# Hybrid S5 and gated-linear-attention trunk on one core: where u is scaled, how q is scaled, and the order of the S5 tables

## The chip, the cores and the metric

One core of a Trainium2 chip runs the kernel. The metric is the device time of one execution in microseconds (us), the median of several runs. TensorE is PE, VectorE DVE, ScalarE ACT, GpSimd POOL; SyncE's queue (SP) issues nearly all DMAs.

## The reference

Two layers on x of 512 tokens by 1024 features, f32, then an RMSNorm:

```python
h = rmsnorm(x, norm_mix)
z = h @ w_in                        # u | q | k | v | g | gate_lr
y = s5(u)                           # 32 groups: 16 channels, 64 complex states
y = gelu(y); y = y * sigmoid(y @ w_glu + b_glu)
y_s5 = rmsnorm(y, s5_out_norm)
y_gla = gated_linear_attention(q, k, v, g, gate_lr)   # 4 heads, chunks of 64
x = x + concat(y_s5, y_gla) @ w_out
h = rmsnorm(x, norm_ffn)
x = x + (silu(h @ W1) * (h @ W2)) @ w_ffn_out
```

S5 is a diagonal complex recurrence s_t = a s_(t-1) + B u_t with the output Re(C s_t) + D u_t; D is the skip diagonal `s5_d`. In the attention, q and k are multiplied with exponentials of the summed log gates within a chunk.

## The kernel before

Activations lie with the features on the partitions: x is eight tiles of 128 x 512. The gain of the norm is folded into x; the row factor rstd (one value for each token, R["rstd"]) is multiplied into the results after the projection. Each projection tile (128 outputs by 512 tokens) is 8 blocks of weights by three matmuls (L575), since a product in f32 is made of high and low halves. Weights come in units of 8 blocks: `Weights.ensure` (L156) issues the load on SP (L142), the cast to the high half on ACT (L163, `whi`) and the low half on DVE (L165, `wlo`), two units ahead. There are two buffers of raw weights, so the load of unit v + 2 waits until unit v is split.

The order on PE, ACT and SP is the order in which the program emits (`manual_schedule`); so is the order on DVE in layer 0 up to the v tiles (the region opened at L1139). POOL, and DVE elsewhere, are ordered by the scheduler of the framework by a modelled timeline and by priority.

The mixer of a layer, `mix` (L647), in the order of layer 0:
- `u_pair` (L698): u tiles 0 and 1, the gate's low-rank tile, u tile 2; in the middle of u tile 2 `stats` (L703) makes rstd and rU, rstd's values in the order of S5 (L682). `gate_a` and `gate_c` (L765, L779) make the sums of the log gates.
- u is reordered for S5: `u_copy` (L740) copies 16 blocks of 32 x 128 from PSUM on ACT, then `u_scale` (L737) multiplies with rU on DVE. Tile 3 follows in `u_tile` (L724), with the gate's exponentials (`gate_b`, L791).
- `q_tile` (L802): one multiply with the exponential E (L807), then four of 64 x 256 with rstd (L814) into `qz`, two tiles padded with zeros by POOL (L813). `k_tile`, `g_tile`, `ke_t` follow, then the four v tiles (`v_tiles`, L906), between whose blocks S5 is called through the table at L1161.
- S5 for one tile of u: `s5_fwd` (L829): 8 matmuls with Wk, four DVE multiplies with cosines and sines (L841 to L844), two POOL adds (L846, L847), eight DVE scans (L852). `s5_back` (L859): four DVE multiplies (L866 to L873) and two POOL adds (L869, L874) make sr and sm. `s5_y` (L881): PE matmuls with Tz and Vx, then gelu on ACT (L899).
- `glu`, the S5 part and the attention part of the output projection close the mixer (`TAIL`, L87).

The S5 tables of layer 0 are made beside this in steps. `prep_w` makes Wk: powers of the decay times B, transposed on DVE (L441) and placed by four DMAs each (L446). `prep_v` makes Vx, four complex products on POOL (`cplx`, L404, eight instructions), and Tz with the skip diagonal `idd` (four DVE multiplies of the identity, L498). `prep_rot` makes cosines and sines on POOL (L567 to L572). `bg0` (L1380) says which steps come at which call of `bg`; the calls stand in L708, L730 and L1141 to L1169. Layer 1's tables are made during the feed-forward part of layer 0, its S5 is called from L1109 to L1137, between q, k and g.

All temporary tiles share a pool of NACT = 45 buffers of 128 x 512 (L203).

## Time and profile before

| | us |
|---|---|
| median of three runs | 1160.08 (1159.53 to 1160.54) |
| the profiled execution, its own time | 1159.86 |
| its span, first to last instruction | 1158.1 |
| busy: PE | 1110.1 |
| busy: DVE | 706.2 |
| busy: ACT | 485.6 |
| busy: POOL | 331.9 |

The span is what the profile's rows cover; 1.76 us of the execution's time lie around it. Matmuls overlap each other and their ends are modelled, so a busy PE is not one at its peak. The mixer of layer 0 takes the first 210 us or so, that of layer 1 lies around 605 to 790 us.

### The profile page before, as it was taken

The page shows a single profiled execution, that of the slowest core. Times are in us where ns is not written, and L with a number is a line of the kernel's source. Part 1 is how long each engine was busy: PE and PEld are TensorE (multiplying, and loading weights), DVE is VectorE, ACT ScalarE, POOL GpSimd, SP SyncE. Part 2 cuts the span into 40 slices and gives each one's busy share as a digit, 9 for nine tenths or more (in the row PEclk, how much of TensorE's full clock was granted, in tenths as well). Part 3 has the DMA queues.
Part 4 walks back from the last instruction along what each step waited for, and adds up shares of the span by engine and source line. Part 5 has one row for each costly group of instructions (what it writes and reads, how often), then busy time and mean ns, then how long its engine had stood idle before and what let it go on. Part 6 is the DMA issues. An engine that isn't in the chain of part 4 may idle for free.

```text
span 1158.1 us, 13973 instructions
## 1 busy us (share of the span) xinstructions
PE 1110.1 (96%) x5316; PEld 913.9 (79%) x5316; DVE 706.2 (61%) x947; ACT 485.6 (42%) x844; POOL 331.9 (29%) x322
## 2 busy tenths in 40 slices
PE   8789779999999999999999799999999999999997
PEld 5568658888888888888887688888888888888886
DVE  7996976866454454564466994686545444444454
ACT  6853458443232232432358653745323222222243
POOL 6899544546000052065030440352000000000003
PEclk9899889999999999999999999999999999999999
...
GB/s 211 55 112 126 37 37 37 92 130 116 103 109 100 137 91 101 82 109 91 93 104 41 73 61 85 56 91 94 107 100 85 106 99 102 91 91 109 91 91 73
DMA packets 64099, 107.72 MB, mean 93 GB/s; under 512 B 37408, under 2 KB 38304, under 8 KB 64032
## 3 DMA queue, kind: packets, MB, share of 16 engines
...
q8 instruction: 42, 0.69, 0.2%
q10 hardware_dynamic: 144, 0.26, 0.1%
...
## 4 chain that ended last, share of the span: by engine, by line
PE 79%; DVE 12%; ACT 3%; issue 2%; POOL 2%; DMA 1%; SPq 1%; DVEq 0%; POOLq 0%; ACTq 0%
PE fg L576 7%; PE fg L577 7%; PE fg L578 7%; PE fu L578 7%; PE fu L576 7%; PE fu L577 7%; PE fo L578 7%; PE fo L576 7%; PE fo L577 7%; DVE ro L852 2%; DVE wlo L165 2%; ACT U L745 1%; DVE qz L814 1%; DMA wrr<-in_wr_dram 1%; DMA raw<-in_wst_dram 1%
## 5 line engine op out<-in xcount | busy, mean ns | idle before, releaser
L165 DVE TENSOR_TENSOR wlo<-raw,whi 128x1024 fp32r<-128x1024 f32 x182 | 242.2, 1333 | 113.2 <-ACT whi L163 112.0
L163 ACT CAST whi<-raw 128x1024 fp32r<-128x1024 f32 x183 | 191.8, 1050 | 280.0 <-PE fo L577 116.9
L602 POOL TENSOR_TENSOR sq_fin<-sq_fin 128x512 f32<-128x512 f32 x5 | 6.5, 1296 | 341.8 <-ACT sq_fin L598 341.8
L1237 DVE TENSOR_TENSOR fu<-fu,rs_ffn 128x512 f32<-128x512 f32 x44 | 30.4, 691 | 116.7 <-PE fu L578 113.9
L1254 DVE TENSOR_TENSOR xall<-xall,fo 128x512 f32<-128x512 f32 x78 | 53.1, 686 | 61.9 <-PE fo L578 61.7
L1234 DVE TENSOR_TENSOR fg<-fg,rs_ffn 128x512 f32<-128x512 f32 x44 | 30.3, 688 | 34.7 <-PE fg L578 30.8
L1236 ACT ACTIVATE fg<-fg 128x512 f32<-128x512 f32 x44 | 27.7, 629 | 42.5 <-DVE fg L1234 42.4
L899 ACT ACTIVATE y<-y 32x128 f32<-32x128 f32 x128 | 34.4, 269 | 20.9 <-PE y L890 17.3
L1238 DVE TENSOR_TENSOR fu<-fg,fu 128x512 f32<-128x512 f32 x44 | 31.3, 711 | 5.7 <-ACT fg L1236 1.3
L745 ACT COPY U<-u 32x128 f32<-32x128 f32 x128 | 32.9, 257 | 1.5
L852 DVE TENSOR_TENSOR_SCAN ro<-sp_mag,ro 128x128 f32<-128x128 f32 x64 | 28.5, 507 | 6.6 <-POOL ro L846 6.6
L1089 POOL TENSOR_TENSOR xall<-xall,wo 128x512 f32<-128x512 f32 x16 | 25.5, 1613 | 24.0 <-DVE wo L1088 24.0
L407 POOL TENSOR_TENSOR pt<-bc,sp_a1r 128x256 f32<-128x256 f32 x2 | 1.7, 852 | 94.0 <-issue 92.0
L568 POOL TENSOR_TENSOR rt<-rg 128x512 f32<-128x512 f32 x8 | 10.2, 1288 | 59.8 <-ACT rg L548 59.7
L602 POOL TENSOR_TENSOR sq_s<-sq_s,sq_s 128x512 f32<-128x512 f32 x6 | 8.1, 1342 | 64.3 <-ACT sq_s L598 64.3
L869 POOL TENSOR_TENSOR sr<-ro,ro 128x508 f32<-128x508 f32 x8 | 14.6, 1826 | 39.3 <-DVE ro L867 39.3
L602 POOL TENSOR_TENSOR sq_x1nmix<-sq_x1nmix 128x512 f32<-128x512 f32 x7 | 9.2, 1315 | 57.3 <-ACT sq_x1nmix L598 57.3
L890 PE MATMUL y<-sr,Vx 128*128 128x128 f32 x64 | 15.0, 322 | 8.0 <-POOL sr L869 7.8
L890 PE MATMUL y<-sm,Vx 128*128 128x128 f32 x64 | 14.8, 318 | 6.2 <-POOL sm L874 6.2
L888 PE MATMUL y<-U,Tz 128*128 128x128 f32 x64 | 14.9, 320 | 5.5 <-DVE ro L842 5.4
L846 POOL TENSOR_TENSOR ro<-ro,ro 128x512 f32<-128x512 f32 x8 | 10.7, 1344 | 30.8 <-DVE ro L843 30.8
L890 PEld LDWEIGHTS y<-sr,Vx 128*128 128x128 f32 x64 | 11.9, 231 | 8.9 <-POOL sr L869 8.9
...
## 6 DMA issues: line engine op xcount, KB each, us to landing
...
```

The costliest lines, as they stand in the source:

```text
L163: self.nc.scalar.copy(hi, raw)
L165: (self.nc.gpsimd if v in POOL_W else self.nc.vector).tensor_tensor(lo, raw, hi.bitcast(F32), op=ALU.subtract)
L576: nc.tensor.matmul(ps, whi, xh, start=start, stop=False)
L577: nc.tensor.matmul(ps, whi, xl, start=False, stop=False)
L578: nc.tensor.matmul(ps, wlo, xh, start=False, stop=stop)
L745: nc.scalar.copy(u[32 * t:32 * t + 32, j].rearrange("p (n c) -> p n c", n=NCH), pv[32 * j:32 * j + 32, :, t, :],)
L852: v.tensor_tensor_scan(dst[:, cs], sp["mag4"][:, c:c + 1].to_broadcast([P, P]), src[:, cs], 0.0, M, A)
L890: nc.tensor.matmul(o, Vx[:, pr, part, 1:].rearrange("p a b c -> p (a b c)"), s_[:, cs], start=False, stop=(part == 1),)
L899: nc.scalar.activation(yv[32 * j:32 * j + 32, :, t, :], ps[32 * t:32 * t + 32, j * P:(j + 1) * P].rearrange("p (n c) -> p n c", n=NCH), AF ...
L1237: nc.vector.tensor_tensor(u, pu, rstd[0], op=M)
L1238: nc.vector.tensor_tensor(u, g, u, op=M)
L1254: nc.vector.tensor_tensor(xT[n], xT[n], ps[n], op=A)
```

## The change

- u is scaled at PSUM: `u_scale` multiplies the PSUM tile with rstd on DVE into a new tile `us`, and the 16 ACT copies read `us`. rU is gone. Tiles 0 and 1 are scaled in `stats`, tile 2 after both `gate_c`, tile 3 ahead of `gate_b`.
- q: `gate_d`, called in `q_tile` behind the matmuls, takes the decay of the chunk ends from E and multiplies E with rstd; four instructions then multiply PSUM with 0.125 and E into `qz`. The `qz` tiles are four fixed tiles that are cleared once at startup.
- The skip diagonal is laid out in memory (columns 1024 to 1151 of `s5bc`) and loaded in `prep_load`; `dskip` leaves the small constants.
- The steps of layer 0's tables follow a list of letters, `TABLES` (s small, w Wk, v Vx and Tz, r rotations). The last two pairs of Wk transposes come two calls earlier each; the fourth product of `prep_v` is made on DVE in layer 0.
- S5 of tile 0 is called ahead of the v tiles, and `s5_scan` is a function of its own, called right behind `s5_fwd` at each other place; the S5 adds and small memsets on POOL get high priority. The table of calls between the v blocks and the order behind it are new.
- NACT is 41.

The diff; left out are the renamed columns, the calls of `s5_scan` in layer 1 and the host's layout:

```diff
     pp = ctx.enter_context(tc.tile_pool(name="pp", bufs=1, space=PS))
-    NACT = 45
+    NACT = 41
...
     Tz = cp.tile([P, 16, P], F32, name="Tz")
+    qz = [[cp.tile([P, 4, 2, 64], F32, name=f"qz{hp}{i}") for i in range(2)] for hp in range(2)]
     cosT = cp.tile([P, 16, P], F32, name="cosT")
...
             t = act(f"bc{l}{i}")
-            nc.sync.dma_start(t, s5bc[l][:, 2 * i:2 * i + 2].rearrange("p a b -> p (a b)"))
+            nc.sync.dma_start(t, s5bc[l][:, 512 * i:512 * i + 512])
             bcs.append(t)
-        return bcs, blks or zeros(f"bk{l}")
+        idd = act(f"idd{l}")[:, 0:P]
+        nc.sync.dma_start(idd, s5bc[l][:, 4 * 256:])
+        return bcs, blks or zeros(f"bk{l}"), idd
...
         for n in (1, 2, 3, 4):
-            cplx(e, l, cr, nci, spv(f"a{n}r", l), spv(f"a{n}i", l),
+            cplx(e[n - 1], l, cr, nci, spv(f"a{n}r", l), spv(f"a{n}i", l),
                  halves(Vx[:, :, 0, n]), halves(Vx[:, :, 1, n]), conj=True)
             yield
-        idd = act(f"idd{l}")
-        for b in range(NB):
-            r = slice(32 * b, 32 * b + 32)
-            nc.vector.tensor_tensor(
-                idd[r, 0:P].rearrange("p (a b) -> p a b", a=4),
-                bcast(C("ident")[r, 32 * b:32 * b + 32], [32, 4, 32], 1),
-                bcast(S(l, "dskip")[r, 4 * b:4 * b + 4], [32, 4, 32], 2), op=M,
-            )
-        yield
         ps = psum(f"kt{l}", "aux")
...
-        def unit_rows():
-            rU = R["rU"] = act(f"rU{l}", F32, (P, P))
-            rv = ntc(R["rstd"])
-            for t in range(TS):
-                h = slice(32 * t, 32 * t + 32)
-                nc.vector.tensor_copy(rU[h].rearrange("p (n c) -> p n c", n=NCH), rv[h, :, t, :])
-
-        U = {}
+        U, us = {}, {}
...
                     nc.vector.tensor_tensor(R["r"], R["psr"], R["rstd"], op=M)
-                unit_rows()
+                for b in range(2):
+                    u_scale(b, ps[b])
                 if l == 0:
                     bg()
-                u_evac(0, ps[0])
+                u_copy(0)
                 W.LOOK = 2
...
             gate_a(1)
-            u_copy(1, ps[1])
+            u_copy(1)
             gate_c(0)
             gate_c(1)
-            u_scale(1)
-            u_evac(2, ps2)
+            u_scale(2, ps2)
+            u_copy(2)
...
             ps = dense(lambda k: ("in", k, b * P), f"u{l}{b}")
+            u_scale(b, ps)
             if mid is not None:
                 mid()
-            u_copy(b, ps)
+            u_copy(b)
             if l == 0:
                 bg()
-            u_scale(b)
-
-        def u_evac(b, ps):
-            u_copy(b, ps)
-            u_scale(b)
-
-        def u_scale(b):
-            nc.vector.tensor_tensor(U[b], U[b], bcast(R["rU"], [P, 4, P], 1), op=M)
-
-        def u_copy(b, ps):
+
+        def u_scale(b, ps):
+            t = us[b] = act(f"us{l}{b}")
+            nc.vector.tensor_tensor(t, ps, R["rstd"], op=M)
+
+        def u_copy(b):
             u = act(f"U{l}{b}", F32, (P, 4, P))
-            pv = ntc(ps)
+            pv = ntc(us.pop(b))
             for j in range(4):
...
             nc.scalar.activation(ntc(ee), nct(mn), AF.Exp, scale=1.0 / 16)
+            E[hp] = (e, ei, ee)
+
+        def gate_d(hp):
+            e = E[hp][0]
             d = dec[hp] = cp.tile([P, NCH], F32, tag=f"dec{hp}", name=f"dec{l}{hp}")
             nc.vector.tensor_copy(d, e.rearrange("p (n s) -> p n s", n=NCH)[:, :, 63])
-            E[hp] = (e, ei, ee)
-
-        def q_tile(hp, mid=None):
+            nc.vector.tensor_tensor(e, e, R["rstd"], op=M)
+
+        def q_tile(hp):
             ps = dense(lambda k: ("in", k, O_Q + hp * P), f"q{l}{hp}")
-            if mid is not None:
-                mid()
+            gate_d(hp)
             e = E[hp][0]
-            nc.vector.scalar_tensor_tensor(e, ps, 0.125, e, op0=M, op1=M)
-            qz = [act(f"qz{l}{hp}{i}", F32, (P, 4, 2, 64)) for i in range(2)]
             for i in range(2):
...
                     r = slice(64 * d, 64 * d + 64)
-                    nc.gpsimd.memset(qz[i][r, :, 1 - d], 0.0)
-                    nc.vector.tensor_tensor(
-                        qz[i][r, :, d], e[r, hf].rearrange("p (n t) -> p n t", n=4),
-                        R["rstd"][r, hf].rearrange("p (n t) -> p n t", n=4), op=M,
+                    nc.vector.scalar_tensor_tensor(
+                        qz[hp][i][r, :, d], ps[r, hf].rearrange("p (n t) -> p n t", n=4), 0.125,
+                        e[r, hf].rearrange("p (n t) -> p n t", n=4), op0=M, op1=M,
                     )
-            qd[hp] = qz
+            qd[hp] = qz[hp]
...
             pe = nc.gpsimd
-            pe.tensor_tensor(a1, a1, a2, op=A)
-            pe.tensor_tensor(a3, a3, a4, op=SB)
+            with tc.high_priority():
+                pe.tensor_tensor(a1, a1, a2, op=A)
+                pe.tensor_tensor(a3, a3, a4, op=SB)
+            rot[b] = (a1, a2, a3, a4, co, si)
+
+        def s5_scan(b):
+            a1, a2, a3, a4, co, si = rot[b]
             for dst, src in ((a2, a1), (a4, a3)):
...
                     c = 16 * l + 4 * b + j
-                    v.tensor_tensor_scan(
+                    nc.vector.tensor_tensor_scan(
                         dst[:, cs], sp["mag4"][:, c:c + 1].to_broadcast([P, P]), src[:, cs], 0.0, M, A
                     )
-            rot[b] = (a1, a2, a3, a4, co, si)
...
             sr, sm = act(f"sr{l}{b}"), act(f"sm{l}{b}")
-            nc.gpsimd.memset(v4(sr)[:, :, 0:1], 0.0)
-            nc.gpsimd.memset(v4(sm)[:, :, 0:1], 0.0)
+            pe = nc.gpsimd
+            with tc.high_priority():
+                pe.memset(v4(sr)[:, :, 0:1], 0.0)
+                pe.memset(v4(sm)[:, :, 0:1], 0.0)
             v.tensor_tensor(a1, a2, co, op=M)
             v.tensor_tensor(a3, a4, si, op=M)
-            pe = nc.gpsimd
-            pe.tensor_tensor(
-                v4(sr)[:, :, 1:P], v4(a1)[:, :, 0:P - 1], v4(a3)[:, :, 0:P - 1], op=SB
-            )
+            with tc.high_priority():
+                pe.tensor_tensor(
+                    v4(sr)[:, :, 1:P], v4(a1)[:, :, 0:P - 1], v4(a3)[:, :, 0:P - 1], op=SB
+                )
             v.tensor_tensor(b1, a2, si, op=M)
             v.tensor_tensor(b2, a4, co, op=M)
-            pe.tensor_tensor(
-                v4(sm)[:, :, 1:P], v4(b1)[:, :, 0:P - 1], v4(b2)[:, :, 0:P - 1], op=A
-            )
+            with tc.high_priority():
+                pe.tensor_tensor(
+                    v4(sm)[:, :, 1:P], v4(b1)[:, :, 0:P - 1], v4(b2)[:, :, 0:P - 1], op=A
+                )
             sst5[b] = (sr, sm)
...
             ke_t(1)
+            s5_fwd(0)
             bg()
+            s5_scan(0)
             region.close()
+
+            def s5(b):
+                s5_fwd(b)
+                s5_scan(b)
+
             v_tiles({
-                0: [bg, bg],
-                1: [lambda: s5_fwd(0), bg],
-                2: [lambda: s5_back(0), bg],
-                3: [lambda: s5_fwd(1)],
-                4: [lambda: score(0), lambda: s5_back(1), bg],
-                5: [lambda: s5_y(0), lambda: s5_fwd(2), bg],
-                6: [lambda: s5_y(1), lambda: s5_back(2), lambda: s5_fwd(3)],
-                7: [lambda: score(1), lambda: s5_back(3)],
+                0: [lambda: s5_back(0), bg],
+                1: [lambda: s5(1), bg],
+                2: [lambda: score(0), bg],
+                3: [lambda: s5_back(1), bg],
+                4: [lambda: s5_y(0), lambda: s5(2), bg],
+                5: [lambda: score(1), lambda: s5_back(2), bg],
+                6: [lambda: s5_y(1), lambda: s5(3)],
+                7: [lambda: s5_back(3)],
             })
+            y_split(0)
             s5_y(2)
-            y_split(0)
             y_split(1)
+            g_tile(3)
             y_split(2)
-            g_tile(3)
             s5_y(3)
...
         nc.gpsimd.memset(Tz, 0.0)
+        for t in qz[0] + qz[1]:
+            nc.gpsimd.memset(t, 0.0)
         blks = zeros("bk0")
...
         pw_ = prep_w(0, nc.vector, pl)
-        pv_ = prep_v(0, nc.gpsimd, pl)
+        pv_ = prep_v(0, 3 * [nc.gpsimd] + [nc.vector], pl)
         next(pv_)
...
-        BG_W = (1, 0, 2, 1, 1, 1, 1, 1, 1, 1)
+        TABLES = (
+            "sssvw", "w", "", "ww", "w", "wr", "wwr", "wwr", "wv", "v", "r", "v", "r", "v", "", "v", "v",
+        )
...
             step0[0] += 1
-            if i == 0:
-                drain(small_)
-                next(pv_)
-                next(pw_)
-                return
-            i -= 1
-            for _ in range(BG_W[i] if i < len(BG_W) else 0):
-                next(pw_, None)
-            if i in (2, 3, 10, 12, 13, 14, 15):
-                next(pv_, None)
-            if i in (4, 5, 6, 10, 11):
-                next(rots)
-            if i == 15:
-                drain(pv_)
+            for c in TABLES[i] if i < len(TABLES) else "":
+                next({"s": small_, "v": pv_, "w": pw_, "r": rots}[c], None)
```

## Rows read from the trace of the kernel before

**Rows 1.** The page, first part: busy us, share of the span, instructions.
```profile
PE 1110.1 (96%) x5316; PEld 913.9 (79%) x5316; DVE 706.2 (61%) x947; ACT 485.6 (42%) x844; POOL 331.9 (29%) x322
```

**Rows 2.** Busy time of each engine in three stretches.
```profile
core 0: us, PE busy (x) PEld busy (x) DVE busy (x) ACT busy (x) POOL busy (x), PEclk, DMA share, GB/s
36.00:63.00 27.00, 22.00 (x80) 16.05 (x81) 26.59 (x50) 23.07 (x53) 22.18 (x25) 0.88 0.19 61
104.00:124.00 20.00, 14.69 (x100) 11.71 (x88) 14.72 (x23) 8.42 (x15) 15.68 (x15) 0.98 0.08 27
639.00:680.00 41.00, 33.44 (x181) 28.77 (x180) 40.87 (x69) 22.85 (x59) 19.96 (x20) 0.96 0.19 58
```

**Rows 3.** Timeline, TensorE, 62 to 125 us: three matmuls that waited.
```profile
start us, us, engine line op out<-in xcount [idle before <-releaser]
...
62.38 0.79 PE L578 MATMUL q<-x0h,wlo 128*128 128x512 f32 x1 [2.93 <-DVE wlo L165]
...
71.14 0.50 PE L578 MATMUL k<-x0h,wlo 128*128 128x512 f32 x1 [1.68 <-DVE wlo L165]
...
124.07 0.76 PE L888 MATMUL y<-U,Tz 128*128 128x128 f32 x2 [5.38 <-DVE ro L842]
```

**Rows 4.** Timeline, ScalarE, 30 to 166 us.
```profile
30.74 4.27 ACT L745 COPY U<-u 32x128 f32<-32x128 f32 x16
...
39.39 1.05 ACT L163 CAST whi<-raw 128x1024 fp32r<-128x1024 f32 x1 [3.31 <-DMA raw<-in_wst_dram]
...
45.45 8.59 ACT L745 COPY U<-u 32x128 f32<-32x128 f32 x32
...
55.53 1.05 ACT L163 CAST whi<-raw 128x1024 fp32r<-128x1024 f32 x1
...
67.03 1.05 ACT L163 CAST whi<-raw 128x1024 fp32r<-128x1024 f32 x1
...
71.56 1.06 ACT L163 CAST whi<-raw 128x1024 fp32r<-128x1024 f32 x1 [3.48 <-DMA raw<-in_wst_dram]
...
164.39 0.63 ACT L1001 ACTIVATE th<-g 128x512 f32<-128x512 f32 x1 [2.81 <-DVE g L992]
```

**Rows 5.** Timeline, VectorE, 36 to 75 us, around the gates and the first q tile.
```profile
36.06 0.62 DVE L706 TENSOR_TENSOR rsb<-r,rs_mix 128x512 f32<-128x512 f32 x1
...
58.24 2.37 DVE L738 TENSOR_TENSOR U<-U,rU 128x512 f32<-128x512 f32 x2
...
69.87 1.22 DVE L165 TENSOR_TENSOR wlo<-raw,whi 128x1024 fp32r<-128x1024 f32 x1
...
71.72 3.07 DVE L814 TENSOR_TENSOR qz<-E,rs_mix 64x256 f32<-64x256 f32 x4
```

**Rows 6.** Timeline, VectorE, single prices, and the first S5 multiply.
```profile
44.35 0.42 DVE L407 TENSOR_TENSOR pt<-bc,sp_fr 128x256 f32<-128x256 f32 x1
...
63.92 0.94 DVE L408 TENSOR_TENSOR pt<-bb,sp_a1i 128x256 f32<-128x256 f32 x1
...
99.80 3.95 DVE L498 TENSOR_TENSOR idd<-cst,xall 32x128 f32<-32x128 f32 x4
103.79 0.69 DVE L841 TENSOR_TENSOR ro<-x,cosT 128x512 f32<-128x512 f32 x1
```

**Rows 7.** Timeline, SyncE's queue: the last group of Wk's DMAs, time of issuing.
```profile
96.01 2.71 SPq L446 DMA_DIRECT2D Wk<-wt  x4
```

**Rows 8.** Timeline, GpSimd: startup, and the first S5 add.
```profile
8.83 0.98 POOL L397 MEMSET bk<- 128x512 f32 x2
13.53 6.09 POOL L602 TENSOR_TENSOR sq_x0nmix<-sq_x0nmix 128x512 f32<-128x512 f32 x4 [3.72 <-ACT sq_x0nmix L598]
...
112.49 1.29 POOL L846 TENSOR_TENSOR ro<-ro,ro 128x512 f32<-128x512 f32 x1
```

**Rows 9.** Timeline, VectorE, 113 to 157 us: scans and the last S5 multiply.
```profile
113.81 4.54 DVE L852 TENSOR_TENSOR_SCAN ro<-sp_mag,ro 128x128 f32<-128x128 f32 x4 [4.61 <-POOL ro L846]
...
128.46 3.19 DVE L852 TENSOR_TENSOR_SCAN ro<-sp_mag,ro 128x128 f32<-128x128 f32 x8
...
156.25 0.69 DVE L873 TENSOR_TENSOR rp<-ro,cosT 128x512 f32<-128x512 f32 x1
```

**Rows 10.** Timeline, VectorE, layer 1: a U scale.
```profile
633.86 1.34 DVE L738 TENSOR_TENSOR U<-U,rU 128x512 f32<-128x512 f32 x1 [1.23 <-ACT U L745]
```

More of the change, by code (lines that the diff above doesn't have):

```diff
@@ L50 @@
 for _n, _w in (
-    ("nmix", 8), ("nffn", 8), ("s5n", 4), ("glan", 4), ("bglu", 4), ("bgate", 2), ("dskip", 16),
+    ("nmix", 8), ("nffn", 8), ("s5n", 4), ("glan", 4), ("bglu", 4), ("bgate", 2),
     ("nfin", 8), ("wgate", 256),
@@ L427, in prep_w @@
     def prep_w(l, e, pl):
-        bcs, bk = pl
+        bcs, bk, _ = pl
         bb = act(f"bb{l}")
@@ L483, in prep_v @@
     def prep_v(l, e, pl):
-        bcs, bk = pl
+        bcs, bk, idd = pl
         cr, nci = v3(bcs[1], 0), v3(bcs[1], 1)
@@ L519, in prep_v @@
                 Tz[0:32, sl, 0:32], kv[:, :, 0:32],
-                idd[r, 0:P].rearrange("p (a b) -> p a b", a=4), op=A,
+                idd[r].rearrange("p (a b) -> p a b", a=4), op=A,
             )
@@ L1114, in mix @@
             s5_fwd(1)
+            s5_scan(1)
             k_tile(0)
@@ L1119, in mix @@
             s5_fwd(2)
+            s5_scan(2)
             k_tile(1)
@@ L1123, in mix @@
             s5_fwd(3)
+            s5_scan(3)
             g_tile(0)
@@ L1158, in mix @@
             ke_t(1)
+            s5_fwd(0)
             bg()
+            s5_scan(0)
             region.close()
+            def s5(b):
+                s5_fwd(b)
+                s5_scan(b)
             v_tiles({
[L1162 to L1169 removed]
+                0: [lambda: s5_back(0), bg],
[6 more added lines that the diff above has]
+                7: [lambda: s5_back(3)],
             })
+            y_split(0)
             s5_y(2)
[L1172 removed]
             y_split(1)
+            g_tile(3)
             y_split(2)
[L1175 removed]
             s5_y(3)
@@ L1413, in bg1 @@
                             prep_w(l + 1, nc.gpsimd, side["pl"]),
-                            prep_v(l + 1, nc.gpsimd, side["pl"]),
+                            prep_v(l + 1, 4 * [nc.gpsimd], side["pl"]),
                             prep_rot(l + 1, nc.gpsimd),
@@ L1456, in lay_out @@
     s5bc = np.empty((DEPTH, P, 4, 16, 16), np.float32)
+    skip = np.zeros((DEPTH, P, 4, 32), np.float32)
     for l in range(DEPTH):
@@ L1464, in lay_out @@
         put(l, "bgate", f["gla_b_gate"][l].reshape(2, P).T)
-        put(l, "dskip", np.tile(f["s5_d"][l].reshape(16, 32).T, (TS, 1)))
+        for b in range(NB):
+            for i in range(32):
+                skip[l, 32 * b + i, :, i] = f["s5_d"][l].reshape(NB, 4, 32)[b, :, i]
         s5l[:, 0, l] = gp(f["s5_lam_re"][l])
@@ L1484, in lay_out @@
     putc("reset", (np.arange(L) % 64 != 0)[None])
-    arr = dict(xt=xt, wst=wst, wr=wr, small=small, s5l=s5l, s5bc=s5bc.reshape(DEPTH, P, 4, 256), const=const)
+    arr = dict(xt=xt, wst=wst, wr=wr, small=small, s5l=s5l, const=const)
+    arr["s5bc"] = np.concatenate([s5bc.reshape(DEPTH, P, 1024), skip.reshape(DEPTH, P, P)], 2)
     return {k: np.ascontiguousarray(v, dtype=np.float32) for k, v in arr.items()}
```

## The prediction

> **What bounds the kernel now.** I read the page first: TensorE (PE) is busy for 1110.1 us, 96% of the span [rows 1], so the 48 us of waiting that are left are all that a better order can win, apart from stretches at the lower clock. Next the engines by stretches: in 36 to 63 us the PE works 22.00 of 27.00 us and VectorE (DVE) 26.59; in 104 to 124 the PE works 14.69 of 20.00 [rows 2]. The losses lie in the mixer of layer 0, and DVE sets the pace. Third, the PE in order of time: 2.93 us before the second q tile, 1.68 before the second k tile, both for the low half of a weight unit (wlo, L165), 5.38 at the first y of the S5 chain [rows 3]. After the 2.93 us the next matmul takes 0.79, after the 1.68 us only 0.50 [rows 3]; the granted clock over 36 to 63 is 0.88 [rows 2], a part of it at 1.2 instead of 2.4 GHz. A longer wait so also costs some clock. So layer 0 has two limits: up to about 100 us the order of weight splits on ScalarE (ACT) and DVE; then, until the last S5 multiply at 156.25 + 0.69 = 156.9 [rows 9], the chain of DVE multiplies, GpSimd (POOL) adds and DVE scans. I measure the change by one moment, T: when DVE starts the four S5 multiplies of tile 0, before at 103.79 [rows 6].
>
> **A. u scaled at PSUM: a new wait on ACT.** Before, ACT copies u from PSUM without the row scale: tile 0 from 30.74, tiles 1 and 2 from 45.45 to 54.0 [rows 4]. Afterwards each copy needs a DVE scale first. Tile 0: rsb ends at 36.7 [rows 5], one scale is 0.7 (a PSUM operand and 512 columns, as the S5 multiply of 0.69 [rows 6]), so copy 0 runs from about 37.4 to 41.7. ACT then has two weight casts (2.1), the gates of two halves and copy 1 (4.3). The gates took 5.0, from the end of the cast ahead of them, 40.4, to 45.45 [rows 4]. That ends at 53.1. But the scale of tile 2 is emitted behind the gate scans, where the scale of tiles 1 and 2 starts before, at 58.24 [rows 5]. DVE is full up to there; the parts removed (four copies of rU, one U scale) and added (two scales) nearly cancel. So copy 2 runs 58.6 to 62.9 instead of ending at 54.0: ACT is 8.9 late.
>
> Behind it on ACT stand the bk copies and the cast of unit 6, 55.53 becoming 64.4 [rows 4]. Its low half follows at 65.6 (1.22 [rows 5]) and the PE's second q tile resumes at 66.8, not 62.38: 4.4 lost. Then come the gate exponentials, copy 3 and the cast of unit 7, 67.03 becoming 76.0; unit 7's low half, before at 69.87 [rows 5], starts at 77.1, and the k tile resumes at 78.3, not 71.14. The PE and DVE are now 7.2 late. The next cast waited 3.48 for its DMA [rows 4], so ACT wins some back; the PE does not. This is the price of the part, between 0 (DVE gets tile 2 done early) and 8.9. I take 7.2, the rows followed one by one. It isn't yet a loss in the end: the PE waits 5.38 and more in the S5 stage anyway.
>
> **B. From unit 7 to T on DVE.** (1) The skip diagonal from memory removes four idd multiplies, 3.95 [rows 6]. Its load is one more issue on SyncE's queue, 0.7 as a fourth of 2.71 [rows 7], early at startup, and nothing reads it for 90 us. (2) q: a scale and four multiplies become a scale of E and four multiplies with one PSUM operand. The four took 3.07 at the first q tile [rows 5]; half of 128x512 from PSUM is taken at 0.42 (0.69 for 512 columns, halved and some start). Two tiles: 2 x (3.07 - 1.7) = 2.7 less, bounds 0 and 3.4. The qz memsets move to the start: four at 0.49 (0.98 for two) in POOL's idle 3.72 [rows 8]: nothing. (3) The fourth decay table moves from POOL to DVE: eight instructions at 0.42 alone or 0.94 beside POOL [rows 6], so 3.4 to 7.5; I take 4, because POOL is less full then. POOL loses them, at most 8 x 1.29 [rows 8]. (4) Wk is transposed two slots earlier, so two more groups of four Wk DMAs stand on SyncE's queue ahead of the loads of units 11 and 12. A group is 2.71 [rows 7], 5.4 in all; DVE can wait 0 to 5.4 for the casts behind them; I take 3.
>
> What (2) and (3) cost is about operands. A multiply with one operand in PSUM took 0.69 while POOL was busy; one with both in SBUF took 0.42 or 0.94 [rows 6]. The Trainium skill, SBUF — State Buffer, Who interferes with whom, says that a DVE instruction with two SBUF inputs contends with a GpSimd instruction that reads SBUF, and one with at most one SBUF input does not. The trace agrees with both halves; by that rule the moved table would pay 7.5 whenever POOL is reading, and the sum would be 3.5 later.
>
> T = 103.8 + 7.2 - 3.95 - 2.7 + 4 + 3 = 111.3.
>
> **C. From T to the first scan.** Before 10.0 (113.81 [rows 9] - 103.79): POOL did rotation tables first and began the add at 112.49 [rows 8]. With the tables ordered earlier and the add at high priority it is three multiplies (1.8) and one add (1.29): 3.1. The scan starts at 114.4, 0.6 later than before.
>
> **D. The S5 chain.** Before 43.1 from first scan to last multiply (156.9 - 113.8). The first four scans took 4.54 beside POOL's tables, a later eight 3.19 [rows 9]: 2.9 less. Masks and memsets that stood between S5 steps move out: 0.5 less (0 to 1.5). One wlo (1.2) that lay ahead of the scans now falls among them. 40.9: it ends at 155.3, 1.6 sooner.
>
> **E. The end of the stage.** ACT's tanh of gate tile 3 waited 2.81 for DVE [rows 4], and the last gelu stands behind it on ACT. With y_split(2) behind g_tile(3), DVE reaches that tile sooner. The gelu also has to wait for its own y, so I take about half, 1.5 less (0 to 2.8).
>
> **F. Layer 1.** DVE is full there as well: 40.87 of 41.00 us, while the PE works 33.44 [rows 2]. DVE loses rU, and the U scales move ahead of the crowded part: one, with its 1.23 of waiting for the copy, costs 2.57 [rows 10]. ACT's first copy starts about 1.2 later (two scales). I take 2.5 less, between 1.2 more and 5 less.
>
> The feed-forward parts pass lateness on in full, since the PE hardly waits there. **Sum: -1.6 - 1.5 - 2.5 = -5.6.** The profiled execution took 1159.86, 0.2 below the median of 1160.08, so I forecast 1154.3.
>
> **Rivals.** All turn on T; the change breaks even at T = 111.3 + 5.6 = 116.9.
> (1) The full lead, 1146: part A costs DVE nothing because tile 2's scale is done in time. T = 104.1, and 7.2 more is won, 1147; with E at its end, 1146. For it: S5 is now called before the v tiles. Against: DVE is busy 26.59 of 27 us where it would have to be early [rows 2].
> (2) Slower, 1165: ACT's blocked queue is paid in full. The wait of 8.9 travels on to T, the casts stand behind loads that stand behind both DMA groups (5.4), the moved table pays 7.5 beside POOL and q saves nothing: T = 103.8 + 8.9 - 3.95 + 7.5 + 5.4 = 121.7. That is 4.8 past break-even; with layer 1 at its bad end 3.7 more. It decides from T = 119.2, 0.2% past break-even. For it: casts are on the PE's path twice before 72 us [rows 3], and the pool of buffers is cut from 45 to 41, so that one more tile may wait. Against: ACT is idle 3.48 right behind [rows 4].
> (3) No change, 1160: the scale moves rather than vanishes, so DVE does the same work and what A loses C and D give back; T between 114.6 and 119.2.
>
> **How the numbers follow.** 0.2%, 2.3 us, is about what a measurement here can tell from no change. My forecast (T from 107 to 114.6) gets 0.40, the full lead 0.19, no change 0.15, slower 0.26. Faster is 0.59. The range leaves out a tenth at each side: from 1144, near the full lead with layer 1 at 5 less, to 1166, the slow case with a part of layer 1's bad end.
>
> **What would show it.** Right: ACT idles some 5 us ahead of the 32-row copies of u tile 2, ending on a DVE scale; the waits at the second q and k tiles grow to about 7 and 4 us; POOL's first S5 add follows its multiplies within 2 us; the first eight scans take near 3.2; no idd on DVE; the last S5 multiply comes before 156. Wrong: the q and k waits stay as they are (then the full lead), or T lies past 117 (then slower), or a new wait for a buffer stands in layer 1.

## The result, and the profile after

The changed kernel takes **1173.85 us**, the median of 4 runs (1173.39 to 1175.54), against 1159.80 for the kernel before, measured beside it: a ratio of 1.0124 (95% interval 1.0106 to 1.0141), 14 us slower. Forecast were 1154.3 and a range from 1144 to 1166. The execution profiled below took 1175.54, 1.7 above the median, with a span of 1173.8.

The page's first part, then busy time by stretches (columns as in [rows 2]; the last stretch is layer 1's S5 stage, which begins 13 us later now):

```profile
PE 1118.7 (95%) x5316; PEld 920.6 (78%) x5316; DVE 703.3 (60%) x939; ACT 490.2 (42%) x844; POOL 316.2 (27%) x302
```
```profile
36.00:63.00 27.00, 20.50 (x76) 14.90 (x76) 22.24 (x41) 20.44 (x55) 21.81 (x27) 0.88 0.18 59
63.00:90.00 27.00, 19.98 (x61) 14.79 (x62) 17.60 (x28) 19.69 (x36) 8.08 (x7) 0.72 0.41 93
104.00:124.00 20.00, 14.86 (x126) 12.80 (x125) 15.60 (x20) 4.20 (x6) 13.95 (x16) 0.83 0.39 114
...
640.00:681.00 41.00, 33.93 (x165) 28.93 (x164) 36.40 (x64) 30.89 (x77) 13.37 (x14) 0.89 0.16 52
```
The second stretch in the kernel before:
```profile
63.00:90.00 27.00, 25.20 (x107) 20.11 (x106) 26.70 (x35) 11.72 (x24) 25.90 (x32) 0.96 0.63 129
```

DVE and POOL have less work than before [rows 1], as the change intends, but DVE is no longer full where it was: 22.24 of 27 us against 26.59 [rows 2], and 17.60 against 26.70 in the stretch behind it. It waits, and so does POOL there: 8.08 us busy against 25.90. Two stretches show a granted clock of 0.72 and 0.83, where the kernel before had 0.96 and 0.98 [rows 2].

What VectorE waits for, and who waits with it: ScalarE, then TensorE, then VectorE, each from the timeline of layer 0.

```profile
37.40 4.91 ACT L730 COPY U<-us 32x128 f32<-32x128 f32 x16 [6.55 <-DVE us L723]
...
58.62 4.89 ACT L730 COPY U<-us 32x128 f32<-32x128 f32 x16 [4.50 <-DVE us L723]
...
64.99 1.04 ACT L163 CAST whi<-raw 128x1024 fp32r<-128x1024 f32 x1
...
91.04 1.05 ACT L163 CAST whi<-raw 128x1024 fp32r<-128x1024 f32 x1 [6.86 <-DMA raw<-in_wst_dram]
...
99.59 1.05 ACT L163 CAST whi<-raw 128x1024 fp32r<-128x1024 f32 x1 [7.50 <-DMA raw<-in_wst_dram]
```
```profile
66.09 0.80 PE L570 MATMUL q<-x0h,whi 128*128 128x512 f32 x1 [7.46 <-ACT whi L163]
...
78.36 0.80 PE L570 MATMUL k<-x0h,whi 128*128 128x512 f32 x1 [3.86 <-ACT whi L163]
...
109.77 3.78 PE L818 MATMUL x<-U,Wk 128*128 128x128 f32 x16 [5.14 <-DVE g L984]
```
```profile
64.69 0.71 DVE L444 STREAM_TRANSPOSE wt<-bk 128x512 f32<-128x512 f32 x1 [6.11 <-ACT bk L439]
...
72.48 0.43 DVE L410 TENSOR_TENSOR pt<-bb,sp_a1r 128x256 f32<-128x256 f32 x1 [3.96 <-ACT Ee L782]
...
116.77 0.68 DVE L826 TENSOR_TENSOR ro<-x,cosT 128x512 f32<-128x512 f32 x1
...
120.05 4.30 DVE L842 TENSOR_TENSOR_SCAN ro<-sp_mag,ro 128x128 f32<-128x128 f32 x4 [0.81 <-POOL ro L832]
...
136.48 4.30 DVE L842 TENSOR_TENSOR_SCAN ro<-sp_mag,ro 128x128 f32<-128x128 f32 x4 [1.02 <-POOL ro L832]
...
169.97 0.68 DVE L864 TENSOR_TENSOR rp<-ro,cosT 128x512 f32<-128x512 f32 x1
```

The copies and waits of the first half are those of part A. T is 116.77 and the first scan comes 3.3 us later; but the chain from there to the end of the last multiply, 170.65, lasts 50.6 us, where [rows 9] gave 43.1.

In the profile's terms the miss adds up. Forecast was a span of 1158.1 - 5.6 = 1152.5; it is 1173.8, 21.3 more:

| step | forecast | measured | miss |
|---|---|---|---|
| A, B: T | 111.3 | 116.77 | 5.5 |
| C: T to first scan | 3.1 | 3.28 | 0.2 |
| D: first scan to end of last multiply | 40.9 | 50.6 | 9.7 |
| E: from there to the end of the cast of y tile 3 that feeds the last glu matmuls (before 13.2) | -1.5 | -0.8 | 0.7 |
| F and all behind | -2.5 | +2.8 | 5.3 |

### The profile page after: what moved, and what is told of

Read it like the earlier page. It is cut to its first block, busy times and chain, and to the rows that moved or that the text cites. A ratio compares the mean times of both kernels' runs of the same rounds, so it can differ in the third digit from the quotient of the medians.

```text
span 1173.8 us, 13945 instructions
## 1 busy us (share of the span) xinstructions
PE 1118.7 (95%) x5316; PEld 920.6 (78%) x5316; DVE 703.3 (60%) x939; ACT 490.2 (42%) x844; POOL 316.2 (27%) x302
## 4 chain that ended last, share of the span: by engine, by line
PE 80%; DVE 10%; ACT 5%; POOL 2%; issue 2%; DMA 1%; SPq 1%; DVEq 0%; ACTq 0%; POOLq 0%
PE fg L570 7%; PE fg L571 7%; PE fu L570 7%; PE fg L572 7%; PE fu L572 7%; PE fu L571 7%; PE fo L570 7%; PE fo L572 7%; PE fo L571 7%; DVE ro L842 2%; ACT U L730 2%; DVE wlo L165 1%; PE y L882 1%; PE v L905 1%; PE gl L571 1%
## 5 line engine op out<-in xcount | busy, mean ns | idle before, releaser
L165 DVE TENSOR_TENSOR wlo<-raw,whi 128x1024 fp32r<-128x1024 f32 x182 | 245.4, 1352 | 130.0 <-ACT whi L163 128.6
L730 ACT COPY U<-us 32x128 f32<-32x128 f32 x128 | 37.8, 295 | 13.5 <-DVE us L723 12.0
L561 POOL TENSOR_TENSOR cosT<-rk 128x512 f32<-128x512 f32 x8 | 11.8, 1482 | 73.2 <-ACT rk L543 72.8
L818 PE MATMUL x<-U,Wk 128*128 128x128 f32 x128 | 17.9, 298 | 5.1 <-DVE g L984 5.1
L818 PEld LDWEIGHTS x<-U,Wk 128*128 128x128 f32 x128 | 17.2, 213 | 5.8 <-DVE g L984 5.4
```

Of the source, the lines that this page charges most:

```text
L165: (self.nc.gpsimd if v in POOL_W else self.nc.vector).tensor_tensor(lo, raw, hi.bitcast(F32), op=ALU.subtract)
L730: nc.scalar.copy(u[32 * t:32 * t + 32, j].rearrange("p (n c) -> p n c", n=NCH), pv[32 * j:32 * j + 32, :, t, :],)
L818: nc.tensor.matmul(ps[part][:, j * P:(j + 1) * P], Wk[:, part, 4 * b + j], U[b][:, j], start=True, stop=True,)
```

## The experiments

Two theories were set against each other at first: ACT's wait for the late scale sets the loss (theory 1), or the new order of tables and S5 calls does (theory 2). Kernels are named by their labels. "First scan" and "end" are the first S5 scan of layer 0 and the end of its last S5 multiply; before 113.81 and 156.94.

### u: four kernels

**e1_scale_early**, the changed kernel with one line moved:
```diff
 gate_a(1)
+u_scale(2, ps2)
 u_copy(1)
 gate_c(0)
 gate_c(1)
-u_scale(2, ps2)
 u_copy(2)
```


> The changed kernel with one line moved: tile 2 of u is scaled on DVE ahead of the gate scans instead of behind them, so that ACT need not wait for it. Theory 1 (ACT's wait sets the loss): ACT's idle time ahead of copy 2 (4.5 us) goes, the waits at the second q tile (7.46) and k tile (3.86) fall to about 3 and 2, and with the casts 5 to 7 us earlier the time falls by 5 to 8, to 1166 to 1169. Theory 2 (the new order of tables and S5 calls sets it): the q and k waits fall just so, but T stays near 116.8, because DVE's low halves of units 11 and 12 still wait for loads queued behind Wk's DMAs; time 1172 to 1174.

**e2_u_alone**, the kernel before with the new `u_scale` and `u_copy` and nothing else (the main lines, in short):
```diff
-u_copy(1, ps[1]); gate_c(0); gate_c(1); u_scale(1); u_evac(2, ps2)
+u_copy(1); gate_c(0); gate_c(1); u_scale(2, ps2); u_copy(2)
```


> The kernel before with u scaled at PSUM alone (q, tables, S5 order, skip diagonal and buffers as before). Theory 1: slower by 7 to 10 us, 1167 to 1170, as the casts come 5 to 9 us late and nothing gives it back. Theory 2: the PE's lateness is absorbed by the waits of the S5 stage, 1159 to 1163.

**e4_u_undone**, the changed kernel with the old pair (the diff above turned round in all places, with rU).


> The changed kernel with u as before: copies from PSUM on ACT, then the scale with rU on DVE; all else of the change stays. Theory 1: 1160 to 1164, the 9 us of ACT are back. Theory 2: 1168 to 1174, because loads behind Wk's DMAs, the wait of the first x matmuls for a PSUM buffer (5.14) and the longer S5 chain (50.6 us from first scan to last multiply) stay.

| | median us | ratio, interval | T | first scan | end |
|---|---|---|---|---|---|
| changed | 1173.85 | 1.0124 (1.0106 to 1.0141) | 116.77 | 120.05 | 170.65 |
| e1 | 1167.70 | 1.0069 (1.0054 to 1.0084) | 112.12 | 115.63 | 163.98 |
| e4 | 1169.89 | 1.0089 (1.0074 to 1.0104) | 111.76 | 115.03 | 165.52 |
| e2 | 1164.72 | 1.0042 (1.0027 to 1.0057) | 111.48 | 118.94 | 160.89 |

The wait is the one forecast, and it comes with u alone. ScalarE, then TensorE, of e2:
```profile
58.77 4.89 ACT L736 COPY U<-us 32x128 f32<-32x128 f32 x16 [4.57 <-DVE us L729]
```
```profile
66.24 0.80 PE L576 MATMUL q<-x0h,whi 128*128 128x512 f32 x1 [7.49 <-ACT whi L163]
...
78.26 0.50 PE L576 MATMUL k<-x0h,whi 128*128 128x512 f32 x1 [3.42 <-ACT whi L163]
```
In e1 one emission place brings the q wait back to 2.98 us and 6.2 us of the time, as theory 1 has it; T falls by 4.7, against theory 2. e2 lies between the two theories, e4 in the range of theory 2. So neither has it all: scaling u as in the change costs 4 to 5 us, and about 10 (e4) remain without it. With its scale early, u at PSUM is even 2.2 us better here than u as before (e1 against e4).

### The order: e3, e5, e10, e11

**e3_order_undone**, the changed kernel with the old order; u, q, skip and 41 buffers stay:
```diff
-"sssvw", "w", "", "ww", "w", "wr", "wwr", "wwr", "wv", "v", "r", "v", "r", "v", "", "v", "v",
+"sssvw", "w", "", "wwv", "wv", "wr", "wr", "wr", "w", "w", "w", "r", "r", "v", "v", "v", "v",
-prep_v(0, 3 * [nc.gpsimd] + [nc.vector], pl)
+prep_v(0, 4 * [nc.gpsimd], pl)
...
```
and the old S5 calls among the v tiles, without the priority on POOL.


> The changed kernel with the order parts undone: the old sequence of table steps, the fourth table on POOL, the old calls of S5 and of y_split, no priority on POOL; u at PSUM, q folded, the skip diagonal from memory and 41 buffers stay. Theory 1: still 5 to 9 above before, 1165 to 1169. Theory 2: back to before or below it, 1155 to 1162, since idd and the dearer q multiplies are gone.

It took 1166.91 us, 1.0059 (1.0042 to 1.0075), in the range of theory 1: first scan 121.44, end 161.55. The chain lasts 40.1, though it begins later than the changed kernel's.

**e5_tables_only** parts the two halves of the order (in short):
```diff
-s5_fwd(0); bg(); s5_scan(0)
-v_tiles({0: [s5_back(0), bg], 1: [s5(1), bg], ...})
+bg()
+v_tiles({0: [bg, bg], 1: [s5(0), bg], 2: [s5_back(0), bg], ...})
```
with u as before.


> The changed kernel with u as before and the old places of the S5 calls among the v tiles; the new order of the tables, the fourth table on VectorE, q, skip and the priority stay. With u as before but the new calls it took 1169.9 us. Theory 1 (the order of the tables is what costs: the DMAs of Wk ahead of the weight loads, the table on VectorE): most of the loss stays, 1166 to 1170, and ScalarE's casts go on waiting 5 us and more for their loads around 90 to 110 us. Theory 2 (the new calls cost: VectorE takes up the S5 chain before it has split the weights of the v tile, and the x tiles wait for a PSUM buffer): 1159 to 1163, the first-scan-to-last-multiply stretch back from 50.5 to under 44 us.

It took 1166.37 us (1165.20 to 1167.75), 1.0052 (1.0037 to 1.0067). With the old calls its first scan comes at 121.65, 6.6 later than in e4, yet its end at 161.61 is 3.9 sooner: 40.0 us of chain instead of 50.5. Theory 1 has the time in its range, theory 2 the chain; both orders cost, 3.5 us the calls and about 3 the tables (below). What makes the chain long is seen in DVE's groups between first scan and end: first e5, then e4 (instructions, busy, mean | waiting before them):
```profile
L849 DVE TENSOR_TENSOR_SCAN ro<-sp_mag,ro 128x128 f32<-128x128 f32 x32 | 14.5, 515 | 2.8 <-POOL ro L839 2.8
...
L165 DVE TENSOR_TENSOR wlo<-raw,whi 128x1024 fp32r<-128x1024 f32 x2 | 2.4, 1206 | 0.0
```
```profile
L849 DVE TENSOR_TENSOR_SCAN ro<-sp_mag,ro 128x128 f32<-128x128 f32 x32 | 18.9, 650 | 5.7 <-POOL ro L839 4.7 <-POOL sm L863 1.0
L165 DVE TENSOR_TENSOR wlo<-raw,whi 128x1024 fp32r<-128x1024 f32 x3 | 4.7, 1554 | 0.0
```
The same 32 scans take 4.4 us more, the waits for POOL 2.9 more, the weight splits that fall into the chain 2.3 more: 9.6 of the 10.5.

**e10_g_other_buffers** and **e11_table_pool** each take one suspect from the changed kernel:
```diff
-AUXG = (1, 2)
+AUXG = ()
```


> The changed kernel with gate tiles 1 and 2 in the PSUM buffers of the other tiles and not in those that x needs. Theory 1 (the wait of 5.14 us of the first x for the buffer of a gate tile, and the stretch at the lower clock behind it, are paid in full): first S5 multiply 3 to 6 us earlier than 116.8, 1168 to 1171. Theory 2 (VectorE is at the weight split of the v tile and at the last table in that time anyway, and comes to the S5 multiplies no sooner): 1173 to 1175.


```diff
-prep_v(0, 3 * [nc.gpsimd] + [nc.vector], pl)
+prep_v(0, 4 * [nc.gpsimd], pl)
```


> The changed kernel with the fourth decay table back on GpSimd. Theory 1 (its 5.3 us stand on VectorE's path to the first S5 multiply): that multiply 3 to 5.3 us earlier than 116.8, 1169 to 1171. Theory 2 (VectorE waits in that stretch for loads and for the split of the v tile's weights, so that the table only fills a wait, or GpSimd's own tables come late instead): 1173 to 1176.

1174.51 us (1173.76 to 1175.47) and 1173.87 (1173.05 to 1174.83): nothing, theory 2 in both. In e10 the wait of 5.14 us for a PSUM buffer is gone, but the same matmuls now wait 3.62 for Wk's DMAs, and T is 116.34. In e11 T falls to 113.59, as in its theory 1, but the first scan stays at 119.94. Two conspicuous rows, a wait of 5.14 and 5.3 us of moved work, are worth no time when they are taken away one by one.

### Skip, q and the buffers: e7, e14, e6, e9, e13

**e7_skip_alone**, the kernel before with only the diagonal loaded from memory:
```diff
-    nc.vector.tensor_tensor(
-        idd[r, 0:P].rearrange("p (a b) -> p a b", a=4),
...
+idd = act(f"idd{l}")[:, 0:P]
+nc.sync.dma_start(idd, s5bc[l][:, 4 * 256:])
```


> The kernel before with only the skip diagonal in memory, 45 buffers, q as before. Theory 1 (the four multiplies of 3.95 us lie on VectorE's path to the first S5 multiply): 1155.5 to 1157.5. Theory 2 (what comes last there is GpSimd's tables and the weight splits): 1159 to 1160. If q or the buffers make the 2.7 us behind layer 0, that stretch is 988 here and 990.7 in the kernel with q folded.

1159.88 us, 1.0002 (0.9993 to 1.0011): theory 2. T is 3.65 us earlier, nearly the 3.95 of the four multiplies, and VectorE then waits for POOL:
```profile
100.14 0.69 DVE L830 TENSOR_TENSOR ro<-x,cosT 128x512 f32<-128x512 f32 x1 [0.73 <-POOL rt L564]
103.02 0.69 DVE L831 TENSOR_TENSOR ro<-x,sinT 128x512 f32<-128x512 f32 x1 [2.19 <-POOL sinT L565]
...
113.14 2.85 DVE L845 TENSOR_TENSOR_SCAN ro<-sp_mag,ro 128x128 f32<-128x128 f32 x2 [5.62 <-POOL ro L835]
```
Of the 3.65, 0.67 is left at the first scan. T was not the moment that sets the end.

**e6_q_skip_alone** is e7 with the q part of the change as it stands: folded, the q tiles fixed, 41 buffers. **e14_q_skip_45** is e6 with the q tiles taken from a pool of 45 when they are needed:
```diff
-qz = [[cp.tile([P, 4, 2, 64], F32, name=f"qz{hp}{i}") for i in range(2)] for hp in range(2)]
-NACT = 41
+NACT = 45
...
+qz = [act(f"qz{l}{hp}{i}", F32, (P, 4, 2, 64)) for i in range(2)]
+nc.gpsimd.memset(qz[i][r, :, 1 - d], 0.0)
```
**e9_skip_41** is e7 with nothing but `NACT = 41`.


> The kernel before with q folded and skip in memory, the q tiles in a pool of 45. Theory 1 (the pool made the loss of 3.6 us of the same kernel with 41): 1157 to 1160. Theory 2 (the folded multiplies stand ahead of the low half of a weight unit and of the S5 chain, and cost by themselves): 1161.5 to 1164.

> The kernel before with q folded, the skip diagonal in memory and 41 buffers, nothing else. Theory 1 (q folded is a loss in layer 1, where four multiplies stand ahead of the S5 chain instead of one: +2.7 us behind layer 0, and layer 0 gains nothing it can keep): 1161 to 1163, the time behind the last gelu of layer 0 is 990.7 instead of 987.9. Theory 2 (VectorE's work ahead of the S5 chain sets the pace of layer 0, so 3.95 + 2.7 us less of it shows): 1155 to 1158.

> The kernel before with the skip diagonal in memory and 41 buffers, q as before: between skip alone with 45 buffers (1159.9 us) and q folded and skip with 41 (1163.5). Theory 1 (q folded makes the 3.6 us: more multiplies of VectorE ahead of the low half of a weight unit and ahead of the S5 chain): 1159.5 to 1160.5. Theory 2 (the four buffers fewer make it, as tiles wait for one): 1162 to 1164, with waits on a buffer's last reader in the trace.

| | median us | ratio, interval | end | layer 1: first q to last y |
|---|---|---|---|---|
| e7 | 1159.88 | 1.0002 (0.9993 to 1.0011) | 156.24 | 89.9 |
| e14 | 1161.42 | 1.0016 (1.0006 to 1.0025) | 155.89 | 92.2 |
| e6 | 1163.48 | 1.0031 (1.0020 to 1.0043) | 158.44 | 92.8 |
| e9 | 1168.34 | 1.0075 (1.0061 to 1.0089) | 161.36 | 90.0 |

e14 came out at the lower edge of its theory 2, e6 half a microsecond above its theory 1, and e9 4.3 us above both of its theories. Folding q costs 1.5 us by itself, and the loss lies in layer 1. There the old q tile gave VectorE one multiply ahead of the S5 chain and put the other four off (e7, VectorE, layer 1); the folded one has all four ahead of it (e14):
```profile
655.18 0.66 DVE L796 SCALAR_TENSOR_TENSOR E<-q,E 128x512 f32<-128x512 f32 x1
655.77 0.68 DVE L859 TENSOR_TENSOR ro<-ro,cosT 128x512 f32<-128x512 f32 x1
...
659.31 3.65 DVE L803 TENSOR_TENSOR qz<-E,rs_mix 64x256 f32<-64x256 f32 x4
```
```profile
655.94 1.70 DVE L807 SCALAR_TENSOR_TENSOR qz<-q,E 64x256 f32<-64x256 f32 x4
657.65 0.69 DVE L863 TENSOR_TENSOR ro<-ro,cosT 128x512 f32<-128x512 f32 x1
```
1.70 instead of 0.66 and 3.65 is less work in a worse place: TensorE's wait for the first sum of the next y tile grows from 1.70 to 3.62 us. The stretch from the start of the first q matmul to that of the last y matmul is 89.8 to 90.0 us in every kernel here with the old q (90.6 in e17), whatever its pool, and 92.2 to 92.8 in every one with the folded q. That the place makes the loss is read from these rows; a folded q at another place was not tried.

The pool is a term of its own: 2.1 us with q folded (e6 against e14), 8.5 with the old q (e9 against e7). The row is the second transposed table of Wk, in e14 and in e6:
```profile
62.08 0.70 DVE L443 STREAM_TRANSPOSE wt<-bk 128x512 f32<-128x512 f32 x1
```
```profile
67.44 0.71 DVE L444 STREAM_TRANSPOSE wt<-bk 128x512 f32<-128x512 f32 x1 [5.33 <-DMA Wk<-wt]
```
With fewer buffers its turn falls on one that DMAs of the first table still read. VectorE stands 5.33 us, and the low half that the k tile needs stands behind it: TensorE's wait there grows from 1.68 to 4.37 us. In e9 the same transpose waits 4.51 us and the chain ends 5.1 us later than in e7; the other 3.4 of its 8.5 us lie behind the chain and are not traced to a row.

**e13_buffers_45**, the changed kernel with its q tiles in a pool of 45:
```diff
-NACT = 41
+NACT = 45
...
+qz = [act(f"qz{l}{hp}{i}", F32, (P, 4, 2, 64)) for i in range(2)]
```


> The changed kernel with the four q tiles back in the shared pool, taken when they are needed, and the pool back at 45; q stays folded. Theory 1 (the smaller pool is a large term: with 41 buffers and nothing else but the skip diagonal the kernel before went from 1159.9 to 1168.3 us): 1166 to 1170, VectorE's waits at 64.69 (6.11) and 72.48 us (3.96) shrink, and the stretch behind layer 0's last gelu is 988 instead of 990.7. Theory 2 (the four q tiles hold as many buffers as were taken away, so nothing is won): 1173 to 1175.

1172.54 us (1171.83 to 1172.63), 1.0112 (1.0098 to 1.0126). The wait of 3.96 at 72.48 becomes two of 1.28 and 1.30, the one for ACT at 64.69 stays (6.16). Only 1.3 us by the medians, half a microsecond below theory 2: there ACT is late anyway, and the stretch in layer 1 is still 92.3.

### What can be won: e8, e12, e15 to e18

**e8_skip_prio_end** keeps from the change the skip diagonal, the priority and the order of the end:
```diff
-s5_y(2); y_split(0); y_split(1); y_split(2); g_tile(3)
+y_split(0); s5_y(2); y_split(1); g_tile(3); y_split(2)
+with tc.high_priority():
     pe.tensor_tensor(a1, a1, a2, op=A)
...
```


> The kernel with only the skip diagonal in memory, and with two more parts of the change: GpSimd's S5 adds and memsets at high priority, and gate tile 3 ahead of the third split of y. If the adds stood behind tables on GpSimd (the first one 6.3 us behind its multiplies), they win 2 to 5 us against skip alone: 1153 to 1157. If VectorE's own work fills that time, nothing: within 0.2% of skip alone.

**1157.49 us, 0.9983 (0.9974 to 0.9992)**: faster than both kernels. Its first scan (113.06) and the end of its chain (156.12) are those of e7 (113.14 and 156.24), so the priority wins nothing up to there. The 2.4 us come behind the chain: ACT's tanh of gate tile 3 waits 0.48 us for VectorE instead of 2.81 [rows 4], and the first q matmul of layer 1 starts 2.7 us sooner. That points to the order of the end; the two were not tried apart.

**e12_best** adds u at PSUM with the early scale, **e15_q_skip_prio_end** the folded q in a pool of 45, and **e16_repaired** is the whole change with early scale and that pool.


> The version with only the skip diagonal in memory, the priority and the end's order (1157.5 us), and u scaled at PSUM with the scale of tile 2 ahead of copy 1 and the gate scans, 45 buffers. Theory 1 (only the late place of that scale made u at PSUM a loss: the changed kernel with the scale early was 2.2 us faster than with u as before): 1154.5 to 1156.5. Theory 2 (with the other parts undone ScalarE has no slack for copies that begin 1.2 us later and read from SBUF at 0.295 instead of 0.257 us): 1158 to 1161.

> As the one before it, with the priority of GpSimd's adds and the end's order, which together were worth 2.3 us to the kernel before: under theory 1 of the last expectation 1154.5 to 1157.5 and the fastest so far, under theory 2 1159 to 1162.

> The changed kernel with all its parts, the scale of u tile 2 moved ahead of copy 1, and the q tiles in a pool of 45. Theory 1 (late scale, 6.2 us, and small pool are separate terms): 1160 to 1165, the rest of the loss being the new order. Theory 2 (both are paid in the same wait of VectorE around 64 to 76 us): 1166 to 1169, little below the 1167.7 of the early scale alone.

Their edits are those of e2 with e1 and of e14, on e8, and of e1 with e13, on the changed kernel. 1159.03 us (0.9996, 0.9987 to 1.0005), 1159.34 (0.9999, 0.9990 to 1.0008) and 1167.70 (1.0069, 1.0055 to 1.0083): theory 2 in all three. On e8 u at PSUM costs 1.5 us even when its scale is early, q 1.9, each good to about a microsecond. e16 is no faster than e1 (1167.70 too), so with the scale early the pool costs nothing that can be seen.

**e17_tables_later** and **e18_last_table_later** test the idea behind the new calls, an early start of the chain, on e8. This is e17; e18 has `"r", "", "vr", "v"` there:
```diff
-..., "w", "r", "r", "v", "v", "v", "v",
+..., "w", "", "", "vr", "vr", "v", "v",
```


> The fastest version so far (skip in memory, priority, the end's order; 1157.5 us) with the rotation tables of tiles 2 and 3 emitted behind the first S5 call instead of ahead of it. There VectorE waits 5.62 us for GpSimd's add of tile 0, which stands behind those tables. Theory 1 (GpSimd's queue ahead of the first scan is the limit in this stage): the first scan at 107 to 109 instead of 113.1 us, the last S5 multiply 2 to 5 us sooner, 1153 to 1156. Theory 2 (the chain then runs beside the tables, scans at 4.5 instead of 3.2 for eight or 2.4 for four, and the sums wait for POOL later, as in the changed kernel with the new calls): the first scan sooner but the last multiply within 1.5 us of 155.5, 1156 to 1159.

> The same with only the rotation table of tile 3 behind the first S5 call: theory 1 about half of the gain, 1155 to 1157; theory 2 no difference, 1156.5 to 1158.5.

1157.62 us (0.9983, 0.9974 to 0.9992) and 1157.16 (0.9978, 0.9969 to 0.9986), both within e8's interval. VectorE, first scan and last multiply, of e8 and of e17:
```profile
113.06 4.53 DVE L846 TENSOR_TENSOR_SCAN ro<-sp_mag,ro 128x128 f32<-128x128 f32 x4 [5.62 <-POOL ro L836]
...
155.44 0.68 DVE L868 TENSOR_TENSOR rp<-ro,cosT 128x512 f32<-128x512 f32 x1
```
```profile
108.96 5.12 DVE L846 TENSOR_TENSOR_SCAN ro<-sp_mag,ro 128x128 f32<-128x128 f32 x4 [1.36 <-POOL ro L836]
...
155.27 0.69 DVE L868 TENSOR_TENSOR rp<-ro,cosT 128x512 f32<-128x512 f32 x1
```
The chain begins 4.1 us sooner and ends 0.2 sooner: theory 2 for e17; e18 lies in the range of theory 2, 0.2 above that of theory 1. The tables that no longer stand ahead of it now run beside it.

### The account

Adding the parts in one order gives the whole. Another order would split it otherwise: u alone on the kernel before is about 5.

| added | kernel | median us | step |
|---|---|---|---|
| skip diagonal | e7 | 1159.88 | 0.1 |
| q folded | e14 | 1161.42 | 1.5 |
| q tiles fixed, 41 buffers | e6 | 1163.48 | 2.1 |
| order of tables, fourth table on DVE, priority | e5 | 1166.37 | 2.9 |
| S5 calls and order of the end | e4 | 1169.89 | 3.5 |
| u at PSUM | changed | 1173.85 | 4.0 |

By the spread of the runs the last four steps are good to 1.5 to 2.2 us each, so their order of size is not settled; their sum is.

## Why the prediction was wrong

The step that failed is **D**: 40.9 us for the chain, measured 50.6, which is 9.7 of the 21.3. It is the largest miss, not the only one: without it the time would still lie 4 us above the kernel before, and B and F add 5.5 and 5.3. D took the 43.1 of before, 2.9 less for the scans (its rows give 2.7), 0.5 less for masks and memsets, 1.2 more for one weight split. By VectorE's rows from first scan to last multiply, the scans are 2.2 more; waits for POOL, for which D has no term, 2.9 more; the third split took 2.1. The masks did not leave the chain (eight in both kernels), only 0.5 of their time went; 0.7 are small pieces.

D priced the scans as if POOL's tables were out of the way, and C calls them "ordered earlier". POOL shows the opposite; its first and last rotation multiply before, then the same two after, with the third product of Vx between them:
```profile
81.59 1.12 POOL L567 TENSOR_TENSOR cosT<-rk 128x512 f32<-128x512 f32 x1
...
116.34 1.41 POOL L572 TENSOR_TENSOR sinT<-sinT,rt 128x512 f32<-128x512 f32 x1
```
```profile
82.15 1.06 POOL L561 TENSOR_TENSOR cosT<-rk 128x512 f32<-128x512 f32 x1 [18.84 <-ACT rk L543]
...
102.97 0.62 POOL L410 TENSOR_TENSOR pt<-bc,sp_a3r 128x256 f32<-128x256 f32 x1
...
138.90 1.29 POOL L566 TENSOR_TENSOR sinT<-sinT,rt 128x512 f32<-128x512 f32 x1
```
The first begins no earlier. Before, POOL made the third and nearly all of the fourth product of Vx in the time in which it now stands idle for 18.84 us; the new list puts them from steps 3 and 4 to 8 and 9, and the third runs among the rotation tables. The tables end 22 us later, beside the scans of tiles 0 and 1: of the first four scans of each of these tiles three are slow, and the four take 4.30 us, where tile 1's eight had taken 3.19 [rows 9].

The twenty traces agree on this. Where the tables end before the first scan (e3, e5, e6, e12) the chain takes 40.0 to 40.1 us, D's figure; where they end 3 to 4 us behind it (before, e2, e7, e8, e9, e14, e15, e18) 42.0 to 44.1; where they end 20 to 22 us behind it (e17 and all that have the new calls) 47.0 to 50.7. The new calls do it: POOL idles in e5 too, 13.73 us, but with the old calls its tables end at 116.9; with the new ones (e4) they end at 135.2: S5's adds stand ahead of them on POOL and wait there for VectorE, 4.01 us for the first add and 4.37 for the first sr. D put a chain of 40.9 behind a first scan at 114.4; no kernel here has both.

- **A** was right row by row: copy 2 at 58.62 (forecast 58.6), cast of unit 6 at 64.99 (64.4), TensorE's waits ending at 66.09 and 78.36 (66.8 and 78.3); VectorE's low half of unit 7 starts at 78.34, 1.2 later than forecast. The prediction says "It isn't yet a loss in the end", yet its sum carries all 7.2 of it to the end. By e2 it moves T by 7.7 and is 4.0 at the end of the chain, about 5 in the time.
- **B** with the start that A gives it fell short by 5.5, in four misses of 1.2 to 1.5. The start is 1.2. (1) came as computed. (2) saved 1.2 instead of 2.7: the four multiplies took 1.73, but the scale of E and the decay copies, which stand in this stretch now, took 3.3 for two tiles. (3) took 5.3 instead of 4. (4) cost 4.3 instead of 3: VectorE's two waits for weights behind Wk's groups were 2.52 and 1.64 before, 3.62 and 4.82 after:
```profile
93.45 1.31 DVE L165 TENSOR_TENSOR wlo<-raw,whi 128x1024 fp32r<-128x1024 f32 x1 [2.52 <-ACT whi L163]
...
97.63 1.65 DVE L165 TENSOR_TENSOR wlo<-raw,whi 128x1024 fp32r<-128x1024 f32 x1 [1.64 <-ACT whi L163]
```
```profile
100.68 1.41 DVE L165 TENSOR_TENSOR wlo<-raw,whi 128x1024 fp32r<-128x1024 f32 x1 [3.62 <-ACT whi L163]
...
107.51 1.60 DVE L165 TENSOR_TENSOR wlo<-raw,whi 128x1024 fp32r<-128x1024 f32 x1 [4.82 <-ACT whi L163]
```
SyncE's queue shows why, two groups of eight in a row ahead of single loads. In the first of them the queue itself waits 3.4 us for VectorE's next transposes, and the load stands behind it:
```profile
86.27 8.67 SPq L449 DMA_DIRECT2D Wk<-wt  x8
95.04 0.56 SPq L142 DMA_DIRECT2D raw<-in_wst_dram  x1
95.70 5.72 SPq L449 DMA_DIRECT2D Wk<-wt  x8
```
- **T as the measure** was a fault of its own. e7 moves T by 3.65 and e11 by 3.2 without effect. The break-even at T = 116.9 would call the measured 116.77 no change, and it is 14 us slower.
- **C** was right: 3.28 against 3.1, with POOL's add at 118.72, 0.1 behind its multiplies.
- **E** was right in kind: 2.3 us in e8 (10.9 from the end of the chain to the cast, against 13.2). In the changed kernel only 0.8 of it is left.
- **F** had the wrong sign. rU and the U scales did leave, but by e2 that alone wins nothing in layer 1's stretch (89.8 us), and the folded q goes ahead of the S5 chain there; it is 2.4 of the 2.8 us lost.
- The pool, named only in the slower rival, had no term in the sum; e9 shows that four buffers can cost 8.5 us.
- **Rivals.** The slower one came true in sign, with A's wait as one of its causes, but its T of 121.7 did not come and A is only 4 of the 14 us. The full lead asked for a scale done in time: e1 does that, and it is 8 us slower than before, so its other terms fail as well. The signs I had named split in the same way: those of A and C and the missing idd came, those of D (eight scans near 3.2, last multiply before 156) did not; T past 117, the sign for slower, just failed to come.
- The remark that a longer wait costs some clock holds for the stretch at 0.72. It does not hold wait by wait: after waits of 2.96 to 2.97 us at the second q tile the next matmul takes 0.50 us in e8 and e14, 0.80 in e7.

What is left open: no run has the new calls with the old list, or without the priority on POOL, so whether the calls alone would push the tables back as far is not shown.
